# Four numbers of a head schedule: an earlier load, a later scaling, wider spacing of x tiles, in a trunk of gated DeltaNet and HGRN2 heads

## The chip, the cores and the metric

The kernel runs on one core of a Trainium2 chip (trn2). The metric is the device time of one execution in microseconds (us). The engines are called PE (TensorE, matmuls), PEld (its weight loads, which overlap with PE), DVE (VectorE), ACT (ScalarE), POOL (GpSimd) and SP (SyncE, which issues the DMAs here).

## The reference

The kernel computes one layer of a hybrid decoder trunk for 2048 tokens of width 1024 in float32. Eight heads of width 128 work on one input projection: four of gated DeltaNet, four of HGRN2. Their outputs go through one output projection; then come a squared-ReLU MLP of width 4096 and a gated per-layer embedding, with RMS norms around each. The change lies in the heads, and what it touches is this:

```python
def gated_delta_rule_chunked(q, k, v, g, beta):      # chunks of 64 tokens
    gc = jnp.cumsum(g, axis=-1)                       # the running sums of the decay
    decay = jnp.exp(jnp.where(causal, gc[..., :, None] - gc[..., None, :], -jnp.inf))
    lmat = jnp.einsum('bhncd,bhnsd->bhncs', k_beta, k) * decay
    a_mat = jnp.eye(c, dtype=jnp.float32) + jnp.where(strict, lmat, 0.0)
    u = solve(v_beta)                                 # triangular, with a_mat
    w = solve(k_beta * jnp.exp(gc)[..., None])
    qg = q * jnp.exp(gc)[..., None]
    k_tail = k * jnp.exp(gc[..., -1:] - gc)[..., None]
    chunk_decay = jnp.exp(gc[..., -1])
    def step(s, inp):                                 # from chunk to chunk
        v_new = u_n - jnp.einsum('bhcd,bhde->bhce', w_n, s)
        o = jnp.einsum('bhcd,bhde->bhce', qg_n, s) + jnp.einsum('bhcs,bhse->bhce', qk_n, v_new)
        s = s * cd_n[..., None, None] + jnp.einsum('bhcd,bhce->bhde', kt_n, v_new)
        return s, o

def gated_head_norm(o, w, z):
    o = o * lax.rsqrt(jnp.mean(o * o, axis=-1, keepdims=True) + EPS)
    return o * w.astype(jnp.float32) * jax.nn.silu(z)
```

## The kernel before

Tokens are worked in four quarters of 512 (`QT`, `NQ`). Each float32 product of a projection is three matmuls of rounded halves. In the mixer stage, about the first 1100 us, PE goes through a list of *works*: per quarter one small one for decay and beta, and for each of four head pairs eight projection tiles (k, q, z, v of the DeltaNet head; f, i, q, gate of the HGRN2 head) of 24 matmuls each. A work is cut into three *ticks* (`SPT`) of eight matmuls, so a head pair takes 24 ticks and a quarter (`per_q`) 99.

What the heads compute besides is written as generators: `gdn_mixer`, `hgrn_mixer`, `x_scale` and others. `at(t, gen, offsets)` puts a generator on the `agenda`: at each tick `t + offset` it runs one step, up to its next `yield`. So the tables of offsets set the order in which everything is written down: `A_STEPS` (43 offsets) for `gdn_mixer`, `B_STEPS` (20) for `hgrn_mixer`. For every head but the first of a quarter `A_AHEAD` takes the place of the first two offsets of `A_STEPS`; its offsets are negative and so fall into the head before. The last head of all has tables of its own, `A_LAST` and `B_LAST`.

The order on SP's queue of DMAs is the one in which the code is written (`manual_schedule` for SP around this stage). The order on DVE, ACT and POOL is set by the framework's scheduler, which sees the same instructions and their dependencies. On every engine and queue an instruction waits behind those ahead of it.

The names, with the lines of the profile:

- `gf` (L638): the running sums of a head, one row read from memory to all 128 partitions, 256 KB, in one buffer. From it come `cd` (L647), `tail` (L648, L650) and `e` (L653 on DVE, four exponentials L655 on ACT), and then its own exponential (L656), which q is multiplied with (L701). This is the second step. Its exponentials need a table load of ACT of their own.
- `ud` (four stores, L707), `sys` (its load back, 512 KB, L716): the triangular systems; `pr`, `xs_g` and `fix` (L728 to L746): the solver on DVE, some forty short instructions; `xd_g` (L750) and `xn_g` (L757) carry its result back.
- the chunk loop, four chunks per head, every four ticks: `psa` (PE, L818), `r` (DVE, L820), `psb` (PE, L823), `w_g` (ACT, L825), `psc` (PE, L828), the next state `S` (DVE, L830).
- `finish` (L607 to L622) ends each head of both kinds: the sum of squares goes through `norm_steps` (the row `rd` in memory), `spread_load` reads the row back to all partitions (`rsb`, L257), and `og` is scaled by it (DVE, L620) and stored to `mixd` (SP, L622). The last two are the last two steps of a mixer.
- `x_scale` (L485): for the next quarter, eight tiles of x (`xs`, 256 KB each, L493, two buffers) are loaded, and ACT squares each one step after its load (L498). Two more steps make and store the scale `rd_x`; `load_x` reads it nine ticks before the next quarter.
- `wd` and `sumd` (L1128 to L1139): sums of MLP weights, made in passing.

Of the kernel before, what the change touches and what calls it, by code (L numbers as in the profile page):

```python
# [54 lines left out]

A_STEPS = ((3, 6, 7, 8, 9, 10, 12, 14) + tuple(range(16, 24)) + (24, 26, 28, 30, 32, 34, 36)
           + tuple(o for c in range(38, 54, 4) for o in (c, c + 1.5, c + 2.5))
           + (53, 55, 57, 59, 60, 61, 63, 64))
I_STEPS = (22,)
B_STEPS = (24, 26, 28, 30, 32, 34, 36, 38, 40, 42, 44, 45, 46, 48, 50, 52, 53, 54, 56, 57)  # L60


A_AHEAD = (-8, -6)


A_FIRST = (3, 7, 8, 8, 9, 10, 12, 14) + tuple(range(16, 24)) + (24, 26, 29, 32, 34, 36, 37)
# [30 lines left out]
def trunk(ctx, tc, x, xT, pT, vecs, w_in, w_ab, gdn_a_log, gdn_dt_bias, w_out, w_up, w_down,  # L97
# [73 lines left out]
    def rsqrt(v):  # L171
        G.tensor_tensor(v, v, mhalf, ALU.pow)
# [76 lines left out]
    def spread(m, name):  # L249

        rd = dr.tile([1, QT], F32, name=f"rd_{name}")
        nc.sync.dma_start(rd.rearrange("o (p n) -> (o p) n", n=NC), m)
        return rd
# [13 lines left out]
    def tok(q):  # L267
        return slice(q * QT, (q + 1) * QT)
# [192 lines left out]
    with mixers as mctx:  # L461
# [23 lines left out]
        def x_scale(q):  # L485
            ss2 = sm.tile([P, 2, NC], F32, tag="ss2", name=f"ss2_x{q}")
            rows4 = x[tok(q), :].rearrange("(p c) d -> p c d", c=NC)
            halves, loaded = [(c, a) for c in range(NC) for a in range(2)], []
            for i in range(len(halves) + 1):
                if i < len(halves):  # L490
                    c, a = halves[i]
                    t = m2.tile([P, QT], F32, tag="ld", name=f"xs{q}_{c}_{a}", bufs=2)
                    nc.sync.dma_start(t, rows4[:, c, a * QT : (a + 1) * QT])  # L493
                    loaded.append(t)
                if i:
                    c, a = halves[i - 1]
                    t = loaded.pop(0)
                    S.activation(t, t, AF.Square, accum_out=ss2[:, a, c : c + 1])  # L498
                yield
            ss = sm.tile([P, NC], F32, tag="ss", name=f"ss_x{q}")  # L500
            V.tensor_tensor(ss, ss2[:, 0, :], ss2[:, 1, :], ALU.add)
            V.tensor_scalar(ss, ss, 1.0 / D, EPS, ALU.mult, ALU.add)
            rsqrt(ss)
            yield
            x_r[q] = spread(ss, f"x{q}")
# [505 lines left out]
        def at(t, gen, offsets):  # L1011
            for o in offsets:
                agenda.setdefault(t + o, []).append(gen)

        def call(t, fn):
            def once():
                fn()
                yield
            at(t, once(), (0,))

        STEPS = SPT = 3
        for q in range(NQ):
            works.append((f"ab{q}", "ab", w_ab, q, None, None, None, None))
            for h in range(4):
                g, b = {}, {}
                t = SPT * len(works)
                for j, then in KINDS:
                    works.append((f"{j}_{q}_{h}", f"in{j + h}", w_in[j + h], q, h, then, g, b))
                a_steps, b_steps = (A_LAST, B_LAST) if (q, h) == (NQ - 1, 3) else (A_STEPS, B_STEPS)
                if h:  # L1030
                    a_steps = A_AHEAD + a_steps[2:]
                elif q == 0:
# [52 lines left out]
        def load_x(q):  # L1085

            rsb = spread_load(x_r[q], f"x{q}", m2, "rsx", 1)
            raws = {}

            def load(k):  # L1090
                raws[k] = m2.tile([P, QT], F32, tag="ld", name=f"raw_xt{q}_{k}", bufs=2)
                nc.sync.dma_start(raws[k], xT[blk(k), tok(q)])

            def scale(k):
                V.scalar_tensor_tensor(raws[k], raws[k], col(R_PREMIX + k), rsb, ALU.mult, ALU.mult)

            def ready(k):
                t = ra.tile([P, 2, QT], F32R, tag="ring", name=f"xt{q}_{k}")
                split(t, V, raws.pop(k))
                xts[q].append(t)  # L1100

            xts[q] = []
            for k in (0, 1):
                load(k)
            yield
            for k in (2, 4):
                t = wp.tile([P, 2, QT], F32, tag="raw", name=f"raw_xt{q}_{k}", bufs=2)
                nc.sync.dma_start(t, xT[k * P : (k + 2) * P, tok(q)].rearrange("(k p) t -> p k t", p=P))
                raws[k], raws[k + 1] = t[:, 0], t[:, 1]
            for k in (0, 1):  # L1110
                scale(k)
                ready(k)
                load(k + 6)
                yield
            for k in range(2, KD):
                scale(k)
                if k % 2:
                    yield
            for k in range(2, KD):
                ready(k)  # L1120
                if k % 2:
                    yield
# [20 lines left out]
        per_q = SPT * (1 + 8 * 4)  # L1143
# [1 line left out]
        for g, t in enumerate(starts):  # L1145
            at(t, down_sums(g), (0, 4, 6, 10))
        for q in range(1, NQ):
            at(per_q * (q - 1) + 30, x_scale(q), range(0, 22, 2))
            at(per_q * q, load_x(q), range(-9, 0))
            call(per_q * q, boundary)  # L1150
        for q in range(2):
# [831 lines left out]
```

## Time and profile before

| | |
|---|---|
| median of three runs | 2644.55 us (2642.86 to 2650.25) |
| profiled execution | 2640.8 us |
| its span | 2639.0 us |
| PE busy | 2602.0 us, 99% |
| PEld, DVE, ACT, POOL busy | 81%, 74%, 56%, 5% |
| granted clock of PE | 1.00 in every stretch |
| mean DMA rate | 217 GB/s |

Times in rows of the profile are from the start of the span. A row of the waits gives the engine and line that waited, what it waited for, the us in total, how often, and the longest. A row of the timeline gives start, duration, engine, line, operation, output and inputs, and in brackets the idle time before with what ended it. In names of tiles `g` stands for DeltaNet and `h` for HGRN2; the timeline leaves out the numbers of quarter, head and chunk.

### The profile page before, as it was taken

To read this page: it belongs to the slowest core of one execution; us is meant where nothing else is said; L and a number is where in the kernel's file an instruction comes from. 1 tells how busy PE (TensorE), PEld (TensorE's weight loads), DVE (VectorE), ACT (ScalarE), POOL (GpSimd) and SP (SyncE) were. 2 spreads that over 40 slices of the span, in tenths; PEclk is the share of its full clock that TensorE was granted. 3 is DMA by queue.
4 is the path that set the end of the run, shared out by engine and by line. 5 is a ranking of instruction groups with operands and counts; after the bars stand their busy time and mean duration, and the time that the engine had idled before them with its cause. 6 is when DMAs were issued, how large, how long until landed. Compare 5 with 4: busy or idle time off the path is not lost.

```text
span 2639.0 us, 43910 instructions
## 1 busy us (share of the span) xinstructions
PE 2602.0 (99%) x15593; PEld 2143.6 (81%) x15593; DVE 1964.8 (74%) x4032; ACT 1466.0 (56%) x2991; POOL 137.0 (5%) x147
## 2 busy tenths in 40 slices
PE   8999999999999999999999999999999999999999
PEld 6787788878878888787888888888888888888887
DVE  7778777776777777579988778767877765478775
ACT  7665655465556555566666465555454465565331
POOL 0000000000000000110000000001000001101000
PEclk9999999999999999999999999999999999999999
DMA  8878777767767675774675576665644475677663
GB/s 279 288 243 263 255 270 247 239 221 248 244 201 251 224 235 163 225 214 138 215 234 183 179 234 224 213 212 186 224 145 168 140 245 186 202 252 251 209 219 128
DMA packets 267788, 573.87 MB, mean 217 GB/s; under 512 B 55578, under 2 KB 60152, under 8 KB 250416
## 3 DMA queue, kind: packets, MB, share of 16 engines
q1 hardware_dynamic: 265264, 566.86, 65.0%
q0 software_dynamic: 2304, 4.20, 0.9%
q8 instruction: 123, 2.02, 0.3%
q14 instruction: 97, 0.79, 0.1%
HBM read 410.57 MB, written 160.37 MB: 216 GB/s over the span
## 4 chain that ended last, share of the span: by engine, by line
PE 80%; DVE 7%; DMA 6%; ACT 3%; issue 3%; SPq 1%; POOL 0%; DVEq 0%; ACTq 0%; POOLq 0%
PE d L1208 23%; PE u L1208 23%; PE mm L1174 19%; PE mmg L1208 7%; PE mmo L1057 1%; PE mme L203 1%; DMA xs<-in_x_dram 1%; DMA ud_g<-u_g 1%; DMA cache_in<-w 1%; DMA sys_g<-ud_g 1%; DVE pr_g L744 1%; DVE xs_g L746 0%; DMA wd<-in_w_down_dram 0%; DVE xt L177 0%; PE psc_g L828 0%
## 5 line engine op out<-in xcount | busy, mean ns | idle before, releaser
L1174 PE MATMUL mm<-xt,w 128*128 128x512 f32 x3072 | 786.4, 401 | 2.9 <-DVE acc_vg L569 1.5
L1174 PEld LDWEIGHTS mm<-xt,w 128*128 128x128 f32 x3072 | 552.9, 188 | 109.0 <-ACT w L176 1.9
L1208 PE MATMUL d<-db,da 128*128 128x512 f32 x2688 | 612.9, 389 | 0.0
L1208 PE MATMUL u<-t,wu 128*128 128x512 f32 x2604 | 591.2, 389 | 0.0
L1208 PEld LDWEIGHTS d<-db,da 128*128 128x128 f32 x2688 | 504.5, 188 | 104.7
L1208 PEld LDWEIGHTS u<-t,wu 128*128 128x128 f32 x2604 | 488.8, 188 | 101.5
L230 DVE TENSOR_TENSOR db<-db 128x512 fp32r<-128x512 f32 x224 | 159.5, 712 | 60.6 <-ACT db L229 60.2
L1606 DVE TENSOR_TENSOR u<-u,u 128x512 f32<-128x512 f32 x224 | 150.0, 680 | 52.4 <-PE u L1208 50.9
L229 ACT ACTIVATE db<-db 128x512 fp32r<-128x512 f32 x224 | 141.0, 629 | 65.3 <-DMA db<-hid 60.8
L1208 PE MATMUL mmg<-h2T,wg 128*128 128x512 f32 (+1 forms) x792 | 174.7, 383 | 0.0
L1208 PEld LDWEIGHTS mmg<-h2T,wg 128*128 128x128 f32 x792 | 145.5, 188 | 29.1
L1649 ACT ACTIVATE u<-u 128x512 f32<-128x512 f32 x128 | 80.7, 631 | 152.8 <-DVE u L1606 152.2
L177 DVE TENSOR_TENSOR da<-da 128x512 fp32r<-128x512 f32 x128 | 93.9, 734 | 91.6 <-ACT da L176 91.3
L176 ACT ACTIVATE da<-da 128x512 fp32r<-128x512 f32 x128 | 80.6, 630 | 128.3 <-DMA da<-sumd 110.2
L1208 PE MATMUL mmo<-mixT,w_out 128*128 128x512 f32 x600 | 138.7, 391 | 3.3 <-DVE w_out L177 2.0
L1208 PEld LDWEIGHTS mmo<-mixT,w_out 128*128 128x128 f32 x600 | 112.2, 188 | 28.8 <-DVE w_out L177 3.2
L176 ACT ACTIVATE wu<-a 128x512 fp32r<-128x512 f32 x124 | 75.1, 623 | 54.8 <-DMA a<-in_w_up_dram 51.8
L177 DVE TENSOR_TENSOR wu<-a,wu 128x512 fp32r<-128x512 f32 x124 | 85.7, 694 | 8.8 <-ACT wu L176 8.3
L177 DVE TENSOR_TENSOR da<-dr,da 128x512 fp32r<-128x512 f32 x96 | 68.2, 711 | 22.5 <-ACT da L176 20.9
L1650 ACT ACTIVATE u<-u 128x512 f32<-128x512 f32 x128 | 80.4, 628 | 3.0
L176 ACT ACTIVATE da<-dr 128x512 fp32r<-128x512 f32 x96 | 60.5, 630 | 31.4 <-DMA dr<-in_w_down_dram 25.6
L246 POOL TENSOR_TENSOR acc_y<-acc_y,sq_y 128x512 f32<-128x512 f32 x28 | 37.8, 1349 | 759.4 <-ACT sq_y L245 759.4
(402 smaller groups left out, 3673.3 us busy)
## 6 DMA issues: line engine op xcount, KB each, us to landing
w<-cache_in SPq DMA_DIRECT2D x96, 1024.0 KB
db<-hid SPq DMA_DIRECT2D x224, 256.0 KB
cache_in<-w SPq DMA_DIRECT2D x32, 1024.0 KB
hid<-u SPq DMA_DIRECT2D x128, 256.0 KB
da<-sumd SPq DMA_DIRECT2D x128, 256.0 KB
a<-in_w_up_dram SPq DMA_DIRECT2D x124, 256.0 KB
hid<-ht SPq DMA_DIRECT2D x96, 256.0 KB
dr<-in_w_down_dram SPq DMA_DIRECT2D x96, 256.0 KB
```

The costliest lines, as they stand in the source:

```text
L176: S.activation(t[:, 0], raw, AF.Copy)
L177: eng.tensor_tensor(t[:, 1], raw, t[:, 0], ALU.subtract)
L203: PE.matmul(ps, a, b, start=i == 0, stop=i == n - 1)
L229: S.activation(t[:, 0], plain(t), AF.Copy)
L230: V.tensor_tensor(t[:, 1], plain(t), t[:, 0], ALU.subtract)
L246: eng.tensor_tensor(acc, acc, sq, ALU.add)
L744: V.tensor_tensor(pr[:, :, :, j + 2 :], xs[:, :, None, j + 2 :].broadcast_to([P, GC, 2, i]), sys[:, None, j : j + 2, j + 2 :].broadcast_to ...
L1174: PE.matmul(ps, *terms[i], start=i == 0, stop=i == nt - 1)
L1208: PE.matmul(ps, a, b, start=start, stop=stop)
L1606: V.tensor_tensor(c[new], c[old], ps, ALU.add)
L1649: S.activation(c[k], c[k], AF.Relu)
L1650: S.activation(c[k], c[k], AF.Square)
```

## The change

Four lines of numbers change; nothing is computed otherwise. The load of `gf` for heads 1 to 3 of a quarter goes from offset -8 to -12, which is tick 12 of the head before, instead of tick 16. The scaling by `rsb` and the store of `mixd` go two ticks back for both kinds of heads, while `rsb` is still loaded at 61 and 54. The steps of `x_scale` come every three ticks instead of two.

```diff
@@ -55,12 +55,12 @@
 A_STEPS = ((3, 6, 7, 8, 9, 10, 12, 14) + tuple(range(16, 24)) + (24, 26, 28, 30, 32, 34, 36)
            + tuple(o for c in range(38, 54, 4) for o in (c, c + 1.5, c + 2.5))
-           + (53, 55, 57, 59, 60, 61, 63, 64))
+           + (53, 55, 57, 59, 60, 61, 65, 66))
 I_STEPS = (22,)
-B_STEPS = (24, 26, 28, 30, 32, 34, 36, 38, 40, 42, 44, 45, 46, 48, 50, 52, 53, 54, 56, 57)
+B_STEPS = (24, 26, 28, 30, 32, 34, 36, 38, 40, 42, 44, 45, 46, 48, 50, 52, 53, 54, 58, 59)
-A_AHEAD = (-8, -6)
+A_AHEAD = (-12, -6)
@@ -1145,7 +1145,7 @@
         for q in range(1, NQ):
-            at(per_q * (q - 1) + 30, x_scale(q), range(0, 22, 2))
+            at(per_q * (q - 1) + 30, x_scale(q), range(0, 33, 3))
             at(per_q * q, load_x(q), range(-9, 0))
```

The order on PE stays as it was, instruction for instruction. On SP, in the second quarter during its first head (`ud_g_0`, `sys_g_0`), before; `w_1_0` are reloads of projection weights, 1 MB each, `gf_g_1` is for the second head, and `mixd_2` takes the output of the third head of the quarter before:

```order
L197 DMA w_1_0_3992<-cache_in_1081 128x2048
L707 DMA ud_g_0_4004<-u_g_0_3924 32x4x32 x4
L1139 DMA sumd_0_4009<-wd_0_3631 128x1024
L1139 DMA sumd_1_4011<-wd_1_3632 128x1024
L622 DMA mixd_2_108<-og_g_2_3621 128x512
L716 DMA sys_g_0_4055<-ud_g_0_4004 128x1x1024
L197 DMA w_1_0_4064<-cache_in_1141 128x2048
L638 DMA gf_g_1_4121<-gd_3550 128x512
```

And the same place on SP now:

```order
L197 DMA w_1_0_3992<-cache_in_1081 128x2048
L707 DMA ud_g_0_4003<-u_g_0_3924 32x4x32 x4
L638 DMA gf_g_1_4008<-gd_3550 128x512
L1139 DMA sumd_0_4010<-wd_0_3631 128x1024
L1139 DMA sumd_1_4012<-wd_1_3632 128x1024
L716 DMA sys_g_0_4056<-ud_g_0_4003 128x1x1024
L197 DMA w_1_0_4065<-cache_in_1141 128x2048
L622 DMA mixd_2_108<-og_g_2_3621 128x512
```

The load of `gf` has moved ahead of that of `sys`, and the store of `mixd` behind it and behind a weight reload: a swap of 256 KB for 256 KB.

On ACT, in the second quarter, between chunks 0 and 1 of the first head (`w_g_0_0`, `w_g_0_1`), before; `hk_h`, `vt_g` and `iT_h` belong to this and the next head, `cd_g_2` to `gf_g_2` are the exponentials for the third head:

```order
L825 ACTIVATE w_g_0_0_4826<-psb_g_0_0_4824,cc_g_0_3784 128x128
L941 ACTIVATE hk_h_0_4832<-t_hkh_0_4833 128x512
L740 ACTIVATE vt_g_1_4855<-t_vg_1_4850,inv_g_1_4518 128x128 x4
L498 ACTIVATE xs_2_1_4767,ss_x_4393<-xs_2_1_4767 128x512
L852 ACTIVATE iT_h_1_4889<-mm_1_1_4808 128x256 x2
L498 ACTIVATE xs_3_0_4817,ss_x_4393<-xs_3_0_4817 128x512
L647 ACT_TABLE_LOAD
L647 ACTIVATE cd_g_2_4922<-gf_g_2_4862 128x4
L650 ACTIVATE tail_g_2_4923<-tail_g_2_4923 128x8
L655 ACTIVATE e_g_2_4929<-e_g_2_4929,gcol_3707 128x128 x4
L656 ACTIVATE gf_g_2_4862<-gf_g_2_4862 128x512
L825 ACTIVATE w_g_0_1_4955<-psb_g_0_1_4953,cc_g_0_3784 128x128
```

And now:

```order
L825 ACTIVATE w_g_0_0_4822<-psb_g_0_0_4820,cc_g_0_3782 128x128
L647 ACT_TABLE_LOAD
L647 ACTIVATE cd_g_2_4913<-gf_g_2_4749 128x4
L498 ACTIVATE xs_1_1_4753,ss_x_4393<-xs_1_1_4753 128x512
L941 ACTIVATE hk_h_0_4828<-t_hkh_0_4829 128x512
L740 ACTIVATE vt_g_1_4851<-t_vg_1_4846,inv_g_1_4517 128x128 x4
L852 ACTIVATE iT_h_1_4880<-mm_1_1_4803 128x256 x2
L650 ACTIVATE tail_g_2_4914<-tail_g_2_4914 128x8
L655 ACTIVATE e_g_2_4920<-e_g_2_4920,gcol_3707 128x128 x4
L656 ACTIVATE gf_g_2_4749<-gf_g_2_4749 128x512
L498 ACTIVATE xs_2_0_4813,ss_x_4393<-xs_2_0_4813 128x512
L825 ACTIVATE w_g_0_1_4948<-psb_g_0_1_4946,cc_g_0_3782 128x128
```

The table load and `cd` now stand right behind `w_g_0_0`, the other exponentials behind `iT_h`, and the two squares of x tiles apart from each other.

On DVE, in the second quarter, around `r` of chunk 2 of the head that ends (`r_g_3_2`), before; `pr_g_0` and `xs_g_0` are the solver of the first head, `og_h_3` and `hl_h_3` the end of an HGRN2 head:

```order
L744 TENSOR_TENSOR pr_g_0_4098<-xs_g_0_4099,sys_g_0_4055 128x8x18
L820 SCALAR_TENSOR_TENSOR r_g_3_2_4199<-psa_g_3_2_4197,tail_g_3_2557,vt_g_3_3256 128x128
L746 TENSOR_REDUCE xs_g_0_4099<-pr_g_0_4098 128x4x2
L744 TENSOR_TENSOR pr_g_0_4098<-xs_g_0_4099,sys_g_0_4055 128x8x20
L1131 TENSOR_TENSOR wd_1_4124<-wd_1_4124,wd_0_4123 128x512
L746 TENSOR_REDUCE xs_g_0_4099<-pr_g_0_4098 128x4x2
L612 TENSOR_TENSOR og_h_3_4201<-of_h,zt_gh_3_3459 128x512
L177 TENSOR_TENSOR hl_h_3_4205<-osq_h_3_4202,hl_h_3_4205 128x512
```

And now:

```order
L744 TENSOR_TENSOR pr_g_0_4100<-xs_g_0_4101,sys_g_0_4056 128x8x20
L746 TENSOR_REDUCE xs_g_0_4101<-pr_g_0_4100 128x4x2
L744 TENSOR_TENSOR pr_g_0_4100<-xs_g_0_4101,sys_g_0_4056 128x8x22
L612 TENSOR_TENSOR og_h_3_4201<-of_h,zt_gh_3_3459 128x512
L177 TENSOR_TENSOR hl_h_3_4205<-osq_h_3_4202,hl_h_3_4205 128x512
L1131 TENSOR_TENSOR wd_1_4124<-wd_1_4124,wd_0_4123 128x512
L820 SCALAR_TENSOR_TENSOR r_g_3_2_4199<-psa_g_3_2_4197,tail_g_3_2557,vt_g_3_3254 128x128
```

Two more pairs of solver steps and the three full-width rows `og_h`, `hl_h` and `wd` now stand ahead of `r_g_3_2`; `tail_g_1` and `e_g_1`, which stood inside the solver, stand ahead of it.

## The prediction

> **What bounds the kernel now.** I read the head of the page first, then the engines' busy time by stretch, because the change touches only the mixer stage, and then who waits for what inside that stage.
>
> ```profile
> span 2639.0 us, 43910 instructions
> PE 2602.0 (99%) x15593; PEld 2143.6 (81%) x15593; DVE 1964.8 (74%) x4032; ACT 1466.0 (56%) x2991; POOL 137.0 (5%) x147
> PE 80%; DVE 7%; DMA 6%; ACT 3%; issue 3%; SPq 1%; POOL 0%; DVEq 0%; ACTq 0%; POOLq 0%
> ```
>
> PE is busy for 2602.0 of 2639.0 us, and the chain that ended last runs through PE for 80%. The most that any change of waits can bring is the 37 us in which PE is idle in the whole program. How much of them lies in the mixer stage the stretches say: the first quarter with the start of its stage, the second, the third, the fourth, and the tail in which the last head ends. The columns are the stretch, its length, then PE, PEld, DVE, ACT and POOL busy with the count of instructions, the granted clock, the DMA share and GB/s.
>
> ```profile
> 45.00:345.00 300.00, 292.55 (x2374) 238.96 (x2375) 235.10 (x642) 196.90 (x476) 17.52 (x28) 1.00 0.78 260
> 345.00:591.00 246.00, 243.52 (x2112) 201.12 (x2112) 187.14 (x547) 140.28 (x376) 14.84 (x17) 1.00 0.73 245
> 591.00:837.00 246.00, 241.95 (x2101) 199.15 (x2100) 182.34 (x536) 138.75 (x374) 14.66 (x17) 1.00 0.72 236
> 837.00:1020.00 183.00, 183.00 (x1589) 152.10 (x1588) 134.05 (x389) 97.48 (x267) 10.51 (x12) 1.00 0.71 225
> 1020.00:1110.00 90.00, 87.66 (x582) 71.47 (x582) 57.98 (x108) 51.85 (x99) 9.61 (x10) 1.00 0.61 182
> ```
>
> PE's idle time is 7.45, 2.48, 4.05, 0 and 2.34 us: 16.3 us is the ceiling for a gain here, 0.6% of the time. DVE (78% in the first stretch, 76% in the second) and ACT have room on average; what they do late can cost PE only at single places. The waits of 45 to 1013 us name those places. First PE's, then those of DVE and ACT that the change aims at (engine and line, what is waited for: us in all, times, longest).
>
> ```profile
> PE psc_g L828 <- ACT w_g L825: 1.9, 3, 0.9
> PE at_all L913 <- ACT y_vg L575: 1.7, 2, 1.0
> DVE pr_g L728 <- DMA sys_g<-ud_g: 23.0, 13, 3.1
> DVE og_g L620 <- DMA rsb_g<-rd_g: 18.5, 11, 2.6
> DVE og_h L620 <- DMA rsb_h<-rd_h: 5.4, 5, 2.4
> ACT xs L498 <- DMA xs<-in_x_dram: 11.2, 8, 4.2
> ACT cd_g L647 <- DMA gf_g<-gd: 7.9, 5, 3.2
> ```
>
> So the change aims at 18.5 + 5.4 + 11.2 + 7.9 = 43.0 us of waits for DMAs. None of them is PE's own; of PE's waits only the first row hangs directly on them. This gap is the core of the forecast.
>
> **The x tiles and the exponentials (a gain).** The three waits of PE for w_g have one cause, and the second quarter shows it:
>
> ```profile
> 391.62 0.63 ACT L498 ACTIVATE xs<-xs 128x512 f32<-128x512 f32 x1 [4.16 <-DMA xs<-in_x_dram]
> 392.36 1.28 ACT L647 ACT_TABLE_LOAD   x1
> 395.56 0.35 ACT L825 ACTIVATE w_g<-psb_g,cc_g 128x128 f32<-128x128 f32 x1
> 395.96 0.49 PE L828 MATMUL psc_g<-w_g,kt_g 128*128 128x128 f32 x2 [0.56 <-ACT w_g L825]
> 637.69 0.63 ACT L498 ACTIVATE xs<-xs 128x512 f32<-128x512 f32 x1 [3.36 <-DMA xs<-in_x_dram]
> 642.80 0.49 PE L828 MATMUL psc_g<-w_g,kt_g 128*128 128x128 f32 x2 [0.53 <-ACT w_g L825]
> ```
>
> ACT stands 4.16 us before an x tile, and the table load and the exponentials of the next head (one block, 392.36 to 395.56) are queued behind it and ahead of w_g. PE then waits 0.56 us. A quarter later the same ACT instruction comes 637.69 - 391.62 = 246.07 us after, which is 99 ticks, so a tick is 2.49 us. Between an x tile's load and its square lay 2 ticks, 5.0 us; now 3, 7.5 us, which covers 2.5 of the 4.16 us. In the new order the exponentials no longer stand right behind two x tiles, and half of the block (the table load and cd) stands behind the preceding w_g. Either alone is over 0.56 us. I therefore let all three waits go: **-1.9 us** (bounds -1.9 and 0). The 11.2 us that ACT waits shrink, but the remaining 9.3 cost PE nothing now. The sum of squares of x is done 10 ticks later, at tick 60, and is used from tick 90 of its quarter on: nothing.
>
> **The running sums' load (a loss).** Per head it is one DMA of 256 KB, moved on SP from behind sys to a place between ud and sys. These rows are SP's around it, with what waits behind:
>
> ```profile
> 316.26 2.46 SPq L707 DMA_DIRECT2D ud_g<-u_g  x4
> 321.62 0.32 SPq L622 DMA_DIRECT2D mixd<-og_g  x1
> 324.17 0.53 SPq L716 DMA_DIRECT2D sys_g<-ud_g  x1
> 325.38 0.43 SPq L638 DMA_DIRECT2D gf_g<-gd  x1
> 332.76 0.21 ACT L647 ACTIVATE cd_g<-gf_g 128x4 f32<-128x4 f32 x1 [1.39 <-DMA gf_g<-gd]
> ```
>
> Here gf takes 332.76 - 325.38 = 7.4 us to land. Issued behind ud, at 318.8, it lands at 326.2, before ACT's old place for cd_g and later than DVE could now use it. For sys, 256 KB more ahead are 262,144 bytes at the second stretch's 245 GB/s: 1.07 us. But the store of mixd, also 256 KB, stood there and moves behind, so for the first two heads of a quarter the net is 0. For the third nothing leaves, and the solver, which starts with sys, is 1.07 us later, four times in the program. Its result goes out and comes back as xn, and that PE waits for at one place of sixteen:
>
> ```profile
> PE psp_g L631 <- DMA xn_g<-xd_g: 1.2, 1, 1.2
> ```
>
> I take 0 for it, as at the fifteen others, with 0 and 4 x 1.07 = 4.3 us as bounds.
>
> The order moves more on DVE than the words of the change say. The next head's tail and e stand ahead of the solver, and the solver's steps and some full-width rows now stand ahead of head 3's r_g and S_g:
>
> ```profile
> 329.15 0.28 DVE L728 TENSOR_TENSOR pr_g<-cst,sys_g 128x64 f32<-128x64 f32 x1 [2.28 <-DMA sys_g<-ud_g]
> 333.68 0.16 DVE L648 TENSOR_TENSOR tail_g<-gf_g,gcol 128x4 f32<-128x4 f32 x1
> 333.75 0.69 DVE L653 TENSOR_TENSOR e_g<-gf_g,cst 128x512 f32<-128x512 f32 x1
> 336.15 0.34 DVE L820 SCALAR_TENSOR_TENSOR r_g<-psa_g,tail_g,vt_g 128x128 f32<-128x128 f32 x1
> 336.41 0.30 DVE L746 TENSOR_REDUCE xs_g<-pr_g 128x8 f32<-128x152 f32 x1
> 339.02 0.68 DVE L1132 TENSOR_TENSOR wd<-wd 128x512 f32<-128x512 f32 x1
> 339.88 0.68 DVE L1134 TENSOR_TENSOR wd<-wd,wd 128x512 f32<-128x512 f32 x1
> 328.07 0.38 PE L823 MATMUL psb_g<-r_g,xt_full 128*128 128x128 f32 x2
> 338.31 0.39 PE L823 MATMUL psb_g<-r_g,xt_full 128*128 128x128 f32 x2
> ```
>
> Before, r_g ends at 336.49 and PE uses it at 338.31: 1.82 us to spare. What passes ahead of r_g now is the stretch behind it, 336.41 to 339.88 without L1132's share (339.02 + 0.68 less its overlap, 0.6): 2.9 us. Against that, e (0.69) leaves the stretch: 2.2 net, 0.4 more than the slack. If e, waiting for gf, also holds the solver up by its own 0.69, it is 1.07. If DVE catches up inside its idle 2.28 us before the solver, it is nothing. PE stands still for 0 to 1.07 us; I take 0.2, the half of 0.4, since tail and e now fall into that idle time. The order has six such places, where an r_g goes back by 1.8 us of DVE's work or more (chunks 2 of head 0, 1 and 2 of head 1 and 2 of head 3 in the first quarter, chunk 1 of head 0 in the second and third): 6 x 0.2 = **+1.2 us**, bounds 0 and 6 x 1.07 = 6.4. Below nothing it can't be: what passes r_g is the solver, on which no row of PE above waits.
>
> **The norms' scaling (nothing).** Its DMA, the store of mixd, goes two ticks back on SP; its reader, the output projection, comes long after. The scaling itself hardly moves in DVE's order:
>
> ```profile
> 623.36 0.75 DVE L620 SCALAR_TENSOR_TENSOR og_g<-og_g,cols,rsb_g 128x512 f32<-128x512 f32 x1 [2.26 <-DMA rsb_g<-rd_g]
> 624.87 0.42 ACT L576 ACTIVATE y_vg<-acc_vg 128x256 f32<-128x256 f32 x1 [3.57 <-DVE acc_vg L569]
> ```
>
> This is the one place where the wait for rsb goes through to PE (the row of at_all above): DVE stands 2.26 us, acc_vg behind it is late, then y_vg, then at_all by about 1.0 us. In the new order the same og_g row stands in front of the same acc_vg rows, so this stays: 0, bounds -1.7 (the whole row) and +1.07 (as for a late r_g).
>
> **The sum.** The profiled execution took 2640.8 us, its span and 1.8 around it. -1.9 + 1.2 + 0 = -0.7 gives 2640.1. The median of the three runs is 3.75 above the profiled execution, so the forecast is 2643.9. The terms' bounds, -1.9 - 1.7 = -3.6 and 6.4 + 4.3 + 1.07 = 11.8 with no gain, give 2641 to 2656. The three runs themselves lie 7.4 us apart; 0.3%, 7.9 us, is about what a measurement of this kernel can tell from no change.
>
> **Rival B, much faster.** The 43.0 us of waits are head-of-line: whatever stands behind them comes late, and PE's idle time in the first three stretches, 7.45 + 2.48 + 4.05 = 14.0 us, is the echo. If three quarters of it go, -10.5 us: 2634. For it: PE's waits there are many small ones, with several releasers each. Against it: the two rows quoted are all that leads back to the moved transfers, and the 18.5 us before og_g stay. It decides if DVE really waits less for rsb. A second version of it comes from how full PE is:
>
> ```profile
> L1208 PE MATMUL d<-db,da 128*128 128x512 f32 x2688 | 612.9, 389 | 0.0
> L1208 PEld LDWEIGHTS d<-db,da 128*128 128x128 f32 x2688 | 504.5, 188 | 104.7
> ```
>
> A group that never waits (0.0) loads weights for 504.5 / 612.9 = 82% of its time; the mixer's stretches show 199.15 / 246 = 81%. So PE is as full there as where nothing holds it. The Trainium skill (Perfetto Trace Analysis, Identifying the Most-Contended Engine) says that matmul busy time misleads and that the share of weight loading is the one to read; taken alone, the page's 81% would leave 19% to win, and by the row of d it leaves about one.
>
> **Rival C, slower: gf lands late at the head of two queues.** DVE has tail and e ahead of r_g of chunk 1, ACT has cd ahead of the next head's gates. With the landing at 326.2, tail and e (0.16 and 0.69) end at 327.0, r_g (0.34) at 327.4, and psb of chunk 1 wants it at 328.07: 0.7 us to spare. It decides when a landing exceeds 7.4 + 0.7 = 8.1 us. If the three moved loads of each quarter do so by 1 us, and each holds PE for that, 12 x 1.0 = 12 us: 2656. For it: sys, with twice the bytes, is next behind gf in the queue, and the DMA share is 0.78 in the first stretch. Against it: 7.4 us is long already, and at the other heads ACT waited for only five loads of sixteen. The Trainium skill (DMA: Bandwidth & Descriptors, Queues, rings and completion order) says that an engine consumes descriptors in ring order, which speaks against this change: gf's bytes stand before those for which DVE waits 23.0 us. By the same page's Anatomy of one DMA (2.0 us and the bytes at 436 GB/s) I estimate 2.6 us for 256 KB, and C could not happen; the trace's 7.4 us says that the queue, not the transfer, sets it.
>
> **Rival D, the change does not do what it says.** DVE's scaling keeps its place; if the other waits also only move from one tile to the next, nothing is left: 2644.6.
>
> **Chances.** With the terms near what I took, the forecast 0.56; B 0.16, since its largest wait is the one that the order leaves; C 0.18, since one landing of those seen is 0.7 us from the edge; D 0.10. The range takes in the forecast's own 2641 to 2656, which holds C's value, and reaches to B's, 2634, with about half of B and of C beyond it: 0.17 left out. Faster by over 0.3% is B, 0.16; slower by over 0.3% is C, 0.18; the forecast and D make 0.66.
>
> **What would show it.** Right: PE's row for w_g gone or below 0.5 us; ACT's waits for gf near 0 and for x tiles below 5 us; DVE's waits for rsb still 15 us or more; small new waits of psb_g for r_g, about 1 us in all. B is shown by PE idle below 5 us in the first three stretches, C by DVE's tail_g or e_g waiting for gf with psb_g behind it, several us in all. The forecast is wrong if PE's idle time before 1110 us changes by over 8 us, or if a wait that no row here names takes the first place.

## The result, and the profile after

| | before | after |
|---|---|---|
| median of 12 runs | 2645.44 us (2642.08 to 2652.82) | 2641.14 us (2635.57 to 2645.52) |
| ratio after to before | | 0.9978, 95% interval 0.9969 to 0.9988 |
| the profiled execution's span | 2639.0 us | 2641.4 us |

The change makes the kernel faster by 0.22%, 4.3 us by the medians and 5.8 by the ratio. The two profiled executions stand the other way round: the one of before was faster than all of its 12 timed runs, the one of after slower than the median of its own. What is read from the two traces is therefore a wait and its place; sizes of a few us come from the timed runs.

The engines' busy time of the changed kernel, and the same five stretches as in the prediction (stretch, length, busy time and count of PE, PEld, DVE, ACT, POOL, then granted clock, DMA share, GB/s):

```profile
PE 2601.6 (98%) x15593; PEld 2143.3 (81%) x15593; DVE 1964.7 (74%) x4032; ACT 1464.2 (55%) x2991; POOL 137.2 (5%) x147
45.00:345.00 300.00, 291.68 (x2372) 238.18 (x2371) 236.12 (x646) 197.71 (x475) 18.37 (x31) 1.00 0.77 261
345.00:591.00 246.00, 243.38 (x2110) 200.71 (x2109) 185.65 (x542) 139.37 (x375) 14.70 (x17) 1.00 0.74 245
591.00:837.00 246.00, 241.68 (x2100) 199.23 (x2099) 181.50 (x534) 137.73 (x373) 14.50 (x17) 1.00 0.72 236
837.00:1020.00 183.00, 183.00 (x1593) 152.19 (x1592) 133.69 (x388) 96.95 (x267) 10.97 (x12) 1.00 0.69 223
1020.00:1110.00 90.00, 87.08 (x580) 70.98 (x579) 57.50 (x108) 51.69 (x100) 9.06 (x9) 1.00 0.61 185
```

PE's idle time in them is 8.32, 2.62, 4.32, 0 and 2.92 us, 18.2 in all where it was 16.3. In this pair of executions nothing was gained. The waits inside the mixer stage, 45 to 1013 us, say what has changed all the same:

```profile
PE of_g L631 <- ACT y_qg L578: 2.6, 3, 1.0
PE psa_g L818 <- DVE S_g L830: 2.5, 4, 0.9
PE at_all L913 <- DVE acc_vg L570: 1.5, 1, 1.5
PE at_all L913 <- ACT y_vg L575: 1.0, 1, 1.0
DVE pr_g L728 <- DMA sys_g<-ud_g: 20.5, 12, 3.0
DVE og_g L620 <- DMA rsb_g<-rd_g: 14.3, 8, 3.4
DVE og_h L620 <- DMA rsb_h<-rd_h: 5.4, 5, 1.7
DVE tail_g L648 <- DMA gf_g<-gd: 2.3, 4, 1.0
ACT xs L498 <- DMA xs<-in_x_dram: 8.3, 6, 2.9
```

PE's row for w_g, 1.9 us in three waits before, is gone. ACT's row for gf, 7.9 us, is gone too; in its place DVE waits 2.3 us in four small pieces. ACT waits 8.3 us for x tiles instead of 11.2. DVE waits 19.7 us for rsb instead of 23.9: the scaling did not get free of its row's load. And PE's waits for the state S, 1.1 us in two waits before, are 2.5 us in four; the prediction did not price them.

The place that the prediction showed, ACT between two chunks in the second quarter, on the timeline of after:

```profile
388.34 1.27 ACT L655 ACTIVATE e_g<-e_g,gcol 128x128 f32<-128x128 f32 x4
391.37 0.63 ACT L498 ACTIVATE xs<-xs 128x512 f32<-128x512 f32 x1 [1.24 <-DMA xs<-in_x_dram]
393.60 0.37 ACT L825 ACTIVATE w_g<-psb_g,cc_g 128x128 f32<-128x128 f32 x1 [1.50 <-PE psb_g L823]
396.14 0.38 PE L828 MATMUL psc_g<-w_g,kt_g 128*128 128x128 f32 x2
```

The exponentials are done before the x tile, ACT waits for that tile 1.24 us instead of 4.16, and w_g now waits for PE instead of PE for w_g: it is ready more than 2 us ahead of psc.

At another place an x tile now stands ahead of something that PE waits for. It is the place that the prediction showed for the scaling, near 623 us:

```profile
622.48 0.63 ACT L498 ACTIVATE xs<-xs 128x512 f32<-128x512 f32 x1 [1.45 <-DMA xs<-in_x_dram]
623.11 0.67 ACT L565 ACTIVATE acc_vg<-mm,cols 128x512 f32<-128x512 f32 x1
623.88 0.75 DVE L569 SCALAR_TENSOR_TENSOR acc_vg<-mm,cols,acc_vg 128x509 f32<-128x509 f32 x1 [3.06 <-ACT hist L566]
624.59 0.75 DVE L620 SCALAR_TENSOR_TENSOR og_g<-og_g,cols,rsb_g 128x512 f32<-128x512 f32 x1
627.49 0.68 PE L913 MATMUL at_all<-qk_h,keys_h 128*128 128x128 f32 x4 [1.53 <-DVE acc_vg L570]
```

ACT stands before an x tile whose square has come to stand ahead of acc_vg's first step. DVE gets that step late, no longer waits for og_g's row, and PE waits 1.53 us. Before, DVE stood before og_g here and PE waited 1.04 us. With the x tiles alone ACT has the same order there, and PE waits 1.93 us. How much of these waits the x tile makes is not shown.

### The profile page after: what moved, and what is told of

It is laid out like the page before. It is cut to its first block, busy times and chain, and to the rows that moved or that the text cites. A ratio compares the mean times of both kernels' runs of the same rounds, so it can differ in the third digit from the quotient of the medians.

```text
span 2641.4 us, 43911 instructions
## 1 busy us (share of the span) xinstructions
PE 2601.6 (98%) x15593; PEld 2143.3 (81%) x15593; DVE 1964.7 (74%) x4032; ACT 1464.2 (55%) x2991; POOL 137.2 (5%) x147
## 4 chain that ended last, share of the span: by engine, by line
PE 76%; DMA 10%; DVE 7%; ACT 3%; issue 3%; SPq 1%; POOL 0%; DVEq 0%; ACTq 0%; POOLq 0%
PE d L1208 23%; PE u L1208 23%; PE mm L1174 17%; PE mmg L1208 7%; DMA cache_in<-w 2%; DMA sys_g<-ud_g 1%; PE mme L203 1%; DMA ud_g<-u_g 1%; DMA raw_out<-in_w_out_dram 1%; DMA mixT<-mixd 1%; DMA xs<-in_x_dram 1%; DMA yod<-yo 1%; DVE w L177 1%; DVE pr_g L744 0%; DMA wd<-in_w_down_dram 0%
```

## The experiments

All ratios are to the kernel before on the same chip; 0.001 is 2.6 us. The three theories of the first four runs: the exponentials leave the stretch before w_g (1), the scaling (2), the x tiles (3).

**The load of gf alone.**

```diff
-A_AHEAD = (-8, -6)
+A_AHEAD = (-12, -6)
```

> Only the load of gf goes four ticks sooner; scaling and x tiles as before. Measured for all three parts: ratio 0.9978. Theory 1 (the gain comes from the ACT block of exponentials that no longer holds up w_g): PE's wait for w_g 0.5 us or less instead of 1.9, ACT's wait for gf near 0, ratio 0.9985 to 1.000, since the DVE order puts r of several heads back and returns part. Theory 2 (the gain is made by the norms' scaling): ratio 1.000 or above. Theory 3 (the gain is made by the x tiles): ratio 1.000, PE's wait for w_g stays at 1 us or more.

Measured 0.9967 (0.9954 to 0.9980) from six runs. It was run again for that reason:

> The earlier load of gf alone once more: it had the best ratio, 0.9967 (0.9954 to 0.9980), from six runs only. If the load alone beats the whole change, this gives 0.9965 to 0.9972 again. If the load, the x tiles and the whole change are all worth the same because they take away the same waits, it gives 0.9975 to 0.9985. In its profile PE's wait for w_g is 0.5 us or less either way.

Measured 0.9980 (0.9971 to 0.9989) from 11 runs. The load alone is a gain of 0.2%, as much as the whole change; that it beats the whole change isn't shown. PE's row for w_g in the first of the two profiles (the second has none):

```profile
PE psc_g L828 <- ACT w_g L825: 0.2, 1, 0.2
```

**The scaling alone.**

```diff
-           + (53, 55, 57, 59, 60, 61, 63, 64))
+           + (53, 55, 57, 59, 60, 61, 65, 66))
-B_STEPS = (24, 26, ..., 52, 53, 54, 56, 57)
+B_STEPS = (24, 26, ..., 52, 53, 54, 58, 59)
```

> Only the scaling and the store of mixd go two ticks back. Theory 1: ratio 1.000 (0.9995 to 1.0005), since DVE's order leaves the scaling nearly where it was and nothing waits for the store; DVE's waits for rsb still 15 us or more, PE's wait for w_g still 1.9 us. Theory 2: DVE's waits for rsb fall to 12 us or less, PE idle before 1110 us falls by 3 us or more, ratio 0.998 to 0.9985. Theory 3: ratio 1.000.

Measured 1.0018 (1.0009 to 1.0026): none of the theories, it is slower. DVE's waits for rsb did fall (11.6 and 3.5 us), and it did not help. The loss has a place. On ACT and PE in the first quarter, second head, chunk 1, first before, then with the scaling alone:

```profile
205.09 1.06 ACT L176 ACTIVATE w<-raw 128x1024 fp32r<-128x1024 f32 x1 [6.18 <-DMA cache_in<-w]
206.06 0.35 ACT L825 ACTIVATE w_g<-psb_g,cc_g 128x128 f32<-128x128 f32 x1
206.97 1.28 ACT L647 ACT_TABLE_LOAD   x1
```

```profile
208.01 1.06 ACT L176 ACTIVATE w<-raw 128x1024 fp32r<-128x1024 f32 x1 [7.27 <-DMA cache_in<-w]
209.09 1.28 ACT L647 ACT_TABLE_LOAD   x1
210.60 1.26 ACT L655 ACTIVATE e_g<-e_g,gcol 128x128 f32<-128x128 f32 x4
212.28 0.35 ACT L825 ACTIVATE w_g<-psb_g,cc_g 128x128 f32<-128x128 f32 x1
212.69 0.79 PE L828 MATMUL psc_g<-w_g,kt_g 128*128 128x128 f32 x2 [3.94 <-ACT w_g L825]
```

In both, ACT stands 6 to 7 us before the split of a raw weight, whose buffer is still being stored. Before, w_g comes right behind the split. With other offsets, ACT's order has the table load and the exponentials between the two, and their 3.2 us come on top of a wait that had used up w_g's slack: PE stands 3.94 us. It then pays a second time. The same stretch by windows, with the granted clock (the share of full speed that the chip gives PE) in the third column from the end:

```profile
195.00:207.50 12.50, 12.50 (x74) 10.76 (x73) 8.17 (x32) 4.33 (x11) 0.00 (x0) 1.00 0.72 244
207.50:212.60 5.10, 1.24 (x7) 0.72 (x6) 4.76 (x14) 4.56 (x10) 0.00 (x0) 0.95 0.91 309
212.60:217.60 5.00, 4.91 (x19) 4.53 (x20) 2.69 (x8) 2.92 (x5) 0.00 (x0) 0.50 0.76 289
217.60:225.00 7.40, 7.40 (x35) 6.17 (x35) 5.86 (x13) 4.18 (x8) 0.00 (x0) 0.91 0.63 195
```

After the stall the clock is at 0.50 for 5 us and 0.91 over the next 7.4: 2.5 + 0.7 = 3.2 us more. The 0.91 is a mean: in stretches of 1 us the clock is 0.50 up to 218 us and 1.00 from 219 us on. Stall and clock make 7.1 us in this profile; the timed runs give a loss of 2.4 to 6.9 us. That every execution stalls as long is not shown.

**The same scaling in the first quarter alone, and in the other three alone.** The offsets are chosen by quarter; the other kernel has `q > 0` in place of `q == 0`, and the last head of all keeps its own tables:

```diff
+                if q == 0 and (q, h) != (NQ - 1, 3):
+                    a_steps, b_steps = A_STEPS[:-2] + (65, 66), B_STEPS[:-2] + (58, 59)
```

> The later scaling and store of mixd in the first quarter alone; all else as before. In the profile of the later scaling alone PE lost 7.2 us at one place of the first quarter, where the weights are also read raw and stored back. Theory 1 (the loss is made there): ratio 1.0015 to 1.002 as for all quarters, a wait of PE for w_g of over 2 us with a granted clock well below 1 behind it. Theory 2 (the loss is made at every head alike): a quarter of it, 1.0004.

> The later scaling and store of mixd in quarters two to four alone. Theory 1: ratio 1.000, no stall of PE above 2 us in the mixer stage. Theory 2: three quarters of the loss, 1.0013.

Measured 1.0017 (1.0008 to 1.0026) and 1.0003 (0.9994 to 1.0013). The loss is made in the first quarter, as theory 1 said. PE's waits for w_g in the two, and the windows of the first at the same place:

```profile
PE psc_g L828 <- ACT w_g L825: 5.9, 4, 4.2
207.50:212.60 5.10, 1.61 (x7) 1.61 (x8) 4.50 (x13) 5.06 (x12) 0.00 (x0) 0.65 0.88 271
212.60:217.60 5.00, 5.00 (x21) 4.31 (x20) 2.86 (x6) 2.71 (x6) 0.00 (x0) 0.68 0.42 177
```

```profile
PE psc_g L828 <- ACT w_g L825: 2.7, 2, 1.8
```

The first row and the two windows are of the first quarter alone, the last row is of the other three. In the one there is a stall of 4.2 us, and again a clock well below 1 at its end; in the other waits up to 1.8 us, and no loss that can be told from chance.

**The x tiles alone, in all sets and in the first.**

```diff
-            at(per_q * (q - 1) + 30, x_scale(q), range(0, 22, 2))
+            at(per_q * (q - 1) + 30, x_scale(q), range(0, 33, 3))
```

```diff
-            at(per_q * (q - 1) + 30, x_scale(q), range(0, 22, 2))
+            at(per_q * (q - 1) + 30, x_scale(q), range(0, 33, 3) if q == 1 else range(0, 22, 2))
```

> Only the x tiles come every three ticks. Theory 1: part of it, ratio 0.9993, PE's wait for w_g about half of 1.9 us, ACT's wait for x tiles below 8 us. Theory 2: ratio 1.000. Theory 3: ratio 0.998 to 0.9985, PE's wait for w_g gone.

> The wider spacing for the x tiles that are loaded in the first quarter alone (two more sets, in the second and the third quarter, as before). Theory 1 (the gain comes from the first quarter, whose transfers are the densest): ratio 0.998, all of the gain of the x tiles. Theory 2 (the gain comes from the three waits for w_g, one per set): a third of it, 0.9993.

All sets: 0.9979 (0.9969 to 0.9988), as much as the whole change. The first set alone: 0.9991 (0.9980 to 1.0001), between the two expectations and telling neither apart. With all sets wider, PE still has one wait for w_g, in the third quarter:

```profile
PE psc_g L828 <- ACT w_g L825: 1.1, 1, 1.1
```

There ACT still stands 4.23 us before an x tile, with the table load and the exponentials queued behind it and ahead of w_g: the third tick did not cover that wait. With the first set alone the wait near 158 us is gone and those of the later quarters are not; PE waits 2.4 us for w_g there in three waits, more than the 1.9 of before, and the run is no slower for it.

**The whole change again, and without the scaling.** The second kernel has the edits of gf and of the x tiles only.

> The whole change once more, on the same chip as its parts. Every theory expects the ratio measured before, 0.9978 (0.9969 to 0.9988). The sum of the three parts' differences from 1 equals this one's if they don't act on each other; theory 1 expects the two of gf and x tiles to overlap, so that their sum is the larger by some 1 us.

> The earlier load of gf and the wider spacing of x tiles, without the later scaling. If the parts add up: 0.9967 x 0.9979 = 0.9946. If both take away the same waits: 0.9965, as the load of gf alone. Either way below the whole change's 0.998, if the later scaling is a loss beside the other two as well.

Measured 0.9983 (0.9975 to 0.9992) and 0.9980 (0.9971 to 0.9989). The parts do not add up: gf and x tiles each give 0.2% alone and 0.2% together, and the product of the parts (0.9946, or 0.9959 with the second run of gf) lies outside the interval of the two together. And the scaling, a loss of 0.18% alone, shows none beside the other two: 0.9978 and 0.9983 with it, 0.9980 without. The trace of after has the reason at the place of the stall:

```profile
195.33 1.28 ACT L647 ACT_TABLE_LOAD   x1
203.45 1.06 ACT L176 ACTIVATE w<-raw 128x1024 fp32r<-128x1024 f32 x1 [2.73 <-DMA cache_in<-w]
205.15 0.37 ACT L825 ACTIVATE w_g<-psb_g,cc_g 128x128 f32<-128x128 f32 x1 [0.64 <-PE psb_g L823]
```

With gf four ticks sooner the table load and the exponentials are done by 200.7 us, ahead of the split that waits and no longer between it and w_g.

**Where the gain of gf lies, and how many ticks it needs.**

The first quarter alone, and two ticks instead of four:

```diff
-                    a_steps = A_AHEAD + a_steps[2:]
+                    a_steps = ((-12, -6) if q == 0 else A_AHEAD) + a_steps[2:]
```

```diff
-A_AHEAD = (-8, -6)
+A_AHEAD = (-10, -6)
```

> The earlier load of gf for heads 1 to 3 of the first quarter alone. Theory 1 (the gain, like the scaling's loss, is made in the first quarter, where ACT also splits raw weights and waits for their stores): 0.997 to 0.998, all of what the load alone brings, PE's wait for w_g at about 158 us gone and those at about 396 and 643 us still there. Theory 2 (the gain is shared by the waits for w_g of three quarters): a third to a half, 0.9985 to 0.999.

> The load of gf two ticks sooner than before instead of four: on SP it then stands right behind the load of sys, not ahead of it, and r goes back on DVE by 0.7 us at most instead of up to 2.4. Theory 1 (the block of exponentials has only to leave the stretch before w_g; two ticks do that in the first quarter): 0.9965 to 0.998, as with four ticks or better. Theory 2 (the gain needs the whole four ticks, since gf takes up to 7.4 us to land): 0.999 or above, and waits of DVE or ACT for gf of 4 us or more remain.

The first quarter alone: 0.9992 (0.9984 to 1.0001). That leaves out theory 1's 0.997 to 0.998, and is near theory 2's value: unlike the scaling's loss, the gain is not all in the first quarter. PE's wait for w_g near 158 us is gone and those near 396 and 643 us are there, as expected. Two ticks, with gf right behind sys: 0.9989 (0.9980 to 0.9998), between the two expectations and nearer theory 2's. PE's waits for w_g are gone there, as with four ticks, but two others are longer than before (1.1 and 0.9 us then), and ACT waits 15.0 us for gf where it waited 7.9:

```profile
PE psa_g L818 <- DVE S_g L830: 1.9, 4, 0.6
PE psa_g L818 <- DVE pr_g L744: 1.5, 3, 0.8
ACT cd_g L647 <- DMA gf_g<-gd: 15.0, 9, 2.8
```

So the place of gf ahead of sys does no harm that would make two ticks the better choice. A kernel without any wait for w_g thus shows about half of the gain that four ticks show, with other waits of PE longer; the two intervals overlap.

**The kernel before against itself.** No edit.

> The kernel before, unchanged, as if it were a changed one: what the comparison and a second profiled execution tell of chance. Expected ratio 1.000, interval with 1 inside. The first profiled execution of it took 2640.8 us, 2.6 below the median of 29 timed runs; if PE's waits differ between executions, this one shows those for w_g in other sizes (1 to 4 us in all) at the same three places.

Measured 1.0002 (0.9993 to 1.0011). Its profile has a span of 2643.5 us and this row, five waits where the first profile had three of 1.9 us in all:

```profile
PE psc_g L828 <- ACT w_g L825: 3.0, 5, 0.9
```

So the term that the prediction read as 1.9 us is one draw; another execution gives 3.0.

## Why the prediction came out

The measured 2641.14 us lies in the range, 0.1% below the forecast 2643.9, but at the lower end of the forecast's own bounds, 2641 to 2656: -0.7 us was forecast, -4.3 to -5.8 measured. The direction was right and the size six to eight times too small; that the time came so near is in part luck, since the base was 0.9 us too low. By its own steps:

- **The waits for w_g go: right, though not from one cause.** The row is gone in after, 0.3 us in the second run of the change, 0.5 without the scaling, and 0.2 or less with gf early alone. At 396 and 643 us the cause named, exponentials queued behind a late x tile and ahead of w_g, is in the rows. At 157.51 us, the largest of the three, it is not. There ACT did not stand before an x tile; it worked without a wait from 150.45 us, the exponentials first and the x tile among them, to w_g at 157.09. So "one cause" held for two places:

```profile
150.45 1.28 ACT L655 ACTIVATE e_g<-e_g,gcol 128x128 f32<-128x128 f32 x4 [0.40 <-DVE e_g L653]
152.15 0.62 ACT L498 ACTIVATE xs<-xs 128x512 f32<-128x512 f32 x1
157.51 0.49 PE L828 MATMUL psc_g<-w_g,kt_g 128*128 128x128 f32 x2 [0.86 <-ACT w_g L825]
```

  Moving either exponentials or x tiles is worth 0.2% and both together no more, so the two edits relieve something that they share. That it is w_g's waits alone is not shown: with the x tiles alone 1.1 us of them are left and the gain is whole, and with gf two ticks sooner none is left and the gain measured is half.
- **Their size, -1.9 us: too small.** The runs give about -5 us. Part of the difference is that 1.9 was one execution (3.0 in another). The rest I can't place. Over the nine profiled executions that have gf early or x tiles wider in some quarter, PE idles 13.2 to 18.2 us up to 1110 us, 15.5 on average; over three without (before, before again, scaling in later quarters) 16.3, 17.5 and 16.2, 16.7 on average. That is 1.2 us of the 5, and the scatter is as large. (The two with the stall of 4 us have 19.5 and 18.7.) It is not the clock on average: the timed runs of one chip have a mean granted clock of 0.9990 with the change and 0.9990 before. Where the others went stays open.
- **gf's load as a loss, +1.2 us for r: wrong, and this is the step that failed.** r_g did go back on DVE, but PE waited for it nowhere in after. At the place shown in the prediction gf took 4.7 us to land, not 7.4, and r kept most of its slack:

```profile
318.30 0.47 SPq L638 DMA_DIRECT2D gf_g<-gd  x1
323.03 0.17 DVE L648 TENSOR_TENSOR tail_g<-gf_g,gcol 128x4 f32<-128x4 f32 x1 [1.02 <-DMA gf_g<-gd]
328.28 0.27 DVE L728 TENSOR_TENSOR pr_g<-cst,sys_g 128x64 f32<-128x64 f32 x1
337.63 0.34 DVE L820 SCALAR_TENSOR_TENSOR r_g<-psa_g,tail_g,vt_g 128x128 f32<-128x128 f32 x1
339.21 0.39 PE L823 MATMUL psb_g<-r_g,xt_full 128*128 128x128 f32 x2
```

  From the end of r at 337.97 to psb at 339.21 there are 1.24 us, where there were 1.82. Of the 2.2 us that the prediction counted for r's queue, 0.58 reached it. What grew instead is S, late for psa by 2.5 us in four waits (1.8 in the second run of the change; 0.6 and 2.1 in the two with gf alone) against 1.1 and 0.6 in the two profiles of before; the prediction quoted no row for it. With the x tiles alone it is 2.1 us, so it is not gf's move that brings it, or not that alone.
- **The scaling, nothing: right in the sum, by a reason that does not carry.** That DVE's order hardly changes is true, and it was the wrong engine. The same offsets change ACT's order, and alone they cost 0.18%, in one place of the first quarter. I weighed the two moved instructions and not what the scheduler does with the others when two offsets change. At the place near 623 us the wait of PE stayed, as said, but not by og_g's wait for rsb: in after DVE does not wait for rsb there, and what comes late is acc_vg, behind an x tile that the prediction took to cost PE nothing.
- **The base.** The forecast added 3.75 us from the profiled execution to the median of three runs; with 12 runs it is 4.64. The two predicted and measured times alone, 2643.9 and 2641.14, therefore understate the miss by 0.9 us.
- **Rival B** stays out: PE did not lose 10 us of idle time, and the waits for rsb stayed at 19.7 us. **Rival C** is refuted by its own sign: DVE's tail waits 1.0 us at most for gf, and no psb behind it does. The 2.6 us estimated there rest on a fit that the Trainium skill (DMA: Bandwidth & Descriptors, Anatomy of one DMA) gives for DMAs issued from GpSimd; gf's is issued by SP, and at this place it took 4.7 and 7.4 us from issue to use. The ring order that the Trainium skill describes (DMA: Bandwidth & Descriptors, Queues, rings and completion order) did not cost what it might have: DVE's wait for sys went from 23.0 to 20.5 us with gf ahead of it, and read 22.9 and 21.0 with gf's move alone. **Rival D** was half true: on DVE the scaling stands nearly where it stood.
- **The signs listed:** ACT's waits for gf are near 0 as said; those for x tiles were to fall below 5 us and fell to 8.3; those for rsb stayed above 15; small waits grew, for S and not for r.

## What to carry to other kernels

Two edits that relieve the same thing are worth one of them: cost them together, and test each alone before keeping both. Where a scheduler sets an engine's order, an edit of offsets is an edit of every engine's order; look for what it puts between a long wait and the next instruction on the chain, on all engines and not on the one that the edit names. And take the size of a small wait from several executions: here one and the same row read 1.9 and 3.0 us in two profiles of one kernel, and whole spans lay 4.5 us apart.

## What the hardware showed unexpectedly

A stall of PE of about 4 us is paid for twice. After the 3.94 us with the scaling alone the granted clock was 0.50 up to 218 us. In the 4.2 us with the scaling in the first quarter it fell to 0.51 at 209 us, some 2 us after PE had stopped, and came back between 215 and 216 us. Added up over stretches of 1 us, both dips make 6.8 us at half clock. Two matmuls of 128 columns took 0.79 us behind the first of these stalls, and 0.38 at the same line in after's row above. The timed runs agree: the mean granted clock is 0.9978 with the scaling alone and 0.9990 before on the same chip, and 0.0012 of 2649 us is 3.2 us.

A shorter wait can be paid for twice as well. The kernel before, in its second profile, waits 1.90 us at one place of the first quarter, and this is the clock in that wait and behind it:

```profile
128.82:130.72 1.90, 0.00 (x1) 0.00 (x1) 1.75 (x3) 1.55 (x5) 0.00 (x0) 1.00 1.00 410
131.00:134.00 3.00, 3.00 (x22) 2.34 (x19) 1.02 (x4) 1.74 (x6) 0.00 (x0) 0.50 0.90 226
```

By stretches of 1 us this dip makes 3.4 us at half clock, and so does one behind a wait of 1.82 us with gf and the x tiles (at 291 us). Behind waits of 1.93 us (x tiles alone, at 622 us) and 2.85 us (gf in the first quarter, at 1118 us) the clock stayed at 1.00. So the length of one wait does not decide it here; what does is not shown. In after, whose longest wait of PE in the list above was 1.5 us, the clock was 1.00 in all five stretches.

The Trainium skill (TensorE: Matmul & The Clock Gate, Part 1: The HAM clock gate) says that the clock falls to half after an idle window of about 3.4 us and comes back after as long a busy one. The 0.50 and the 3.4 us of the short dips agree with it. The falls behind waits of 1.82 and 1.90 us, the one some 2 us into a stall, and the 6.8 us of the long dips do not come out of it, and here the measurement decides.
